# The first token block's 1/rms moved from the input of the first projection to its outputs

## The chip, the cores and the metric

The kernel is one program on one core of a Trainium2 chip. The metric is the device time of one execution in microseconds (us), the median of the runs shown. Engines are named as in the profile: PE (TensorE matmul) and PEld (its weight loads), DVE (VectorE), ACT (ScalarE), POOL (GpSimd), SP (SyncE, which issues most DMAs; SPq is its queue).

## The reference, cut to what matters

One hybrid decoder layer over 2064 tokens (16 meta tokens and 2048 others) of 1024 features, all in fp32:

```python
h = jnp.concatenate([meta, x], axis=1)
hn = rms_norm(h, norm_mix_g[i])              # h * rsqrt(mean(h*h) + eps) * g
proj = hn @ w_in[i]                          # 1024 -> 4 x 512
b_gate, c_gate, v, u = ...                   # the four groups of 512 columns
conv_out = b_gate * causal_dwconv(c_gate * v, conv_w[i])
ssm_out = s5_group_ssm(u, ...)               # diagonal complex state space, GELU, half-GLU
mixed = concat(rms_norm(conv_out, ...), rms_norm(ssm_out, ...))
h = h + mixed @ w_out[i]
hn = rms_norm(h, norm_ffn_g[i])
up = causal_dwconv(hn @ w_up[i], ...);  a, val = up[:D_FF], up[D_FF:]
h = h + (silu(a) * val) @ w_down[i]
y = rms_norm(h, norm_final_g)[:, N_META:]
```

The factor 1/rms of a token is one number for all its features. So it can be multiplied into `h` ahead of `@ w_in`, or into the columns of the product behind it. In `b_gate * dwconv(c_gate * v)` each of the three factors carries it for its own token.

## The kernel before, in words

**Layout.** Features lie on the 128 partitions (8 groups of 128), tokens along the free dimension. The tokens are cut into six quarters q0 to q5 of 344 tokens (`QL`), two to a block; block 0 is q0 and q1. A quarter of x comes as two halves of four feature groups each (tiles `x_c`, 128x1376, 688 KB, from three buffers with the tag `xt`).

**Products.** Each fp32 operand is split into a high part in the format fp32r and a low part that is the rest (`parts`, L245: ACT copies the high part, DVE subtracts for the low part). A product is then three matmuls per feature group: high x high (L138), weight-high x x-low (L139), weight-low x x-high (L142). Weights are loaded in tiles of 128x1024 (`wr_*`, three buffers) and split into `wh_*` and `wl_*` (four buffers each), two tiles ahead of their use (`Stream`).

**Units.** One weight tile times one block is a unit: 48 matmuls of 128x344 into one of three PSUM buffers of two banks (`unit`, L831). The first unit of a block runs its two quarters one after the other (`by_chunk`), so it can begin with q0 alone. `u_block(b)` (L842) has four units, whose outputs (`pu`) go through ACT (L852) in a strided order into `ut`, and from there to DRAM for the state space. `conv_block(b)` (L859) has four groups j of three units: v (`cv`, copied by ACT to `vs`, L865), c (`cc`, multiplied by `vs` into `cvt` on DVE, L870) and b (`cb`, multiplied on DVE into the convolved `tc`, L883). The order is u_block(0), conv_block(0), u_block(2), u_block(1), conv_block(1), conv_block(2), then the output projections, then the gated MLP over three blocks.

**The norm of a quarter.** `prep_x` (L346) loads the two halves; ACT squares them (`sq_c`, L164); DVE adds them up in three steps (L168 to L170); PE sums over partitions (`st_c`, L188); DVE and POOL form (mean + eps) to the power -1/2 (`sv_c`, `sr_c`, L198 and L199); DVE spreads it on a diagonal (`dg_c`, L203); PE broadcasts it (`sb_c`, L206); ACT copies it to `rs_c` (L211). Then DVE forms x times gain times 1/rms in four instructions per half (`t_c`, L240), ACT copies the high part (`h_c`) and DVE subtracts the low part (`l_c`). `t_c` and `sq_c` share two buffers (tag `sq`).

**The coefficients of the state space.** The generator `coefficients` (L375) computes tables from two loads (`sm`, `bc`) on DVE, in some 300 instructions, many of them on 48 columns; its step is taken four times after every unit of block 0 (`after_unit`, L821), in the order of the program, and is finished after the tenth unit. In it are the matmuls `kps` (L576), 16 transposes (`tp`, L590) that ACT copies out (`tq`, L592) and SP stores to `mat_d`, and after them eight copies `tm` (L623) that are stored there too (L624). `tq` and `tm` share two buffers. When the generator is finished its pool `a0` is released. The pool `xf2`, which takes that space from the right end, holds the split tiles of q4: by the program's addresses the first of them, `h_c4_0` (bytes 207,200 to 212,736 of a partition), lies over the second of the two `tq`/`tm` buffers (bytes 207,104 to 209,152).

**Order of work.** The framework that the kernel is written in orders each engine's instructions ahead of time: an engine issues in a fixed order, in which an instruction that is later in the program stands earlier where the engine would otherwise have nothing ready. `prep` and `ssm` are lists of generators from which one or more steps are taken after each unit. q4 and q5, which u_block(2) needs, are prepared one after the other.

```python
    first = [prep_x(q, hc[0]) for q in range(2)]
    next(first[0])
    stream.fill()
    next(first[1])
    ssm.step(1)
    finish_gens(*first)
    u_block(0, hc[0])
```

Of the kernel before, what the change touches and what calls it, by code (L numbers as in the profile page):

```python
# [11 lines left out]
F32 = mybir.dt.float32  # L12
F32R = mybir.dt.float32r
I32 = mybir.dt.int32
AF = mybir.ActivationFunctionType
ALU = mybir.AluOpType

P = 128
# [4 lines left out]
NJ = 8  # L23
# [5 lines left out]
QL = 344  # L29
NQ = L // QL  # L30
QM = 346
# [5 lines left out]
C_MIX = 0  # L37
# [20 lines left out]
def layer_kernel(ctx, tc, xq, pk, w_in, w_glu, w_out, w_up, w_down, ssm_s, ssm_m, y):  # L58
    nc = tc.nc
    V, S, T, G = nc.vector, nc.scalar, nc.tensor, nc.gpsimd  # L60
# [4 lines left out]
    cp = ctx.enter_context(tc.tile_pool(name="cp", bufs=1))  # L65
# [22 lines left out]
    def col(c):  # L88
        return pv[:, c : c + 1]
# [12 lines left out]
    def f32(ap):  # L102
        return ap.bitcast(F32)

    def two(ap):
        return ap.rearrange("p (c t) -> p c t", c=2)

    def tt(out, a, b, op):
        V.tensor_tensor(out, a, b, op=op)  # L109

    def mul(out, a, b):
        tt(out, a, b, ALU.mult)

    def axpy(out, a, s, b):
        V.scalar_tensor_tensor(out=out, in0=a, scalar=s, in1=b, op0=ALU.mult, op1=ALU.add)  # L115

    def load_weights(src, nk, name):
        raw = wp.tile([P, KD, P], F32, tag="wr", bufs=3, name=f"wr_{name}")
        dma(out=raw[:, :nk, :], in_=src)
        return raw, nk, name  # L120
# [23 lines left out]
    def rhs_of(hs):  # L144
        return lambda k, c: (hs[c][k // 4][0][:, k % 4, :], hs[c][k // 4][1][:, k % 4, :])

    def half_tile(n, name, tag="xt", bufs=3):
        return xp_.tile([P, 4, QM], F32, tag=tag, bufs=bufs, name=name)[:, :, :n]

    def hl_tile(n, name, pool=None, tag="xhl", bufs=8):  # L150
        return (pool or xf).tile([P, 4, QM], F32R, tag=tag, bufs=bufs, name=name)[:, :, :n]
# [7 lines left out]
    def sum_squares(groups, n, name):  # L159

        sqs = []
        for i, a in enumerate(groups):
            sq = half_tile(n, f"sq_{name}_{i}", tag="sq", bufs=2)
            S.activation(sq if len(a.shape) == 3 else sq.rearrange("p k (j c) -> p k j c", j=NJ), a, AF.Square)  # L164
            sqs.append(sq)
        sq = sqs[0]
        if len(sqs) == 2:
            tt(sq, sq, sqs[1], ALU.add)  # L168
        tt(sq[:, 0:2, :], sq[:, 0:2, :], sq[:, 2:4, :], ALU.add)
        tt(sq[:, 0, :], sq[:, 0, :], sq[:, 1, :], ALU.add)  # L170
        return sq[:, 0, :]

    def inv_rms(groups, n, name, out=None):


        s = sum_squares(groups, n, name)
        yield
        yield
        return (yield from inv_rms_of(s, 4 * P * len(groups), n, name, out))

    def inv_rms_of(s, nfeat, n, name, out=None, keep=False):
        sl, starts = slices(n)
        nj = len(starts)
        ps = aux_tile(f"st_{name}")
        terms = s if isinstance(s, list) else [s]
        for j, o in enumerate(starts):
            for i, a in enumerate(terms):
                T.matmul(  # L188
                    ps[:sl, j : j + 1], a[:, o : o + sl], ones[:, 0:1], start=i == 0, stop=i == len(terms) - 1
                )  # L190
        return (yield from inv_rms_at(ps[:sl, :nj], starts, nfeat, n, name, out, keep))
# [53 lines left out]
    def parts(t, hi, lo):  # L245

        S.activation(hi, t, AF.Copy)  # L247
        tt(lo, t, f32(hi), ALU.subtract)
# [4 lines left out]
    def load_halves(loads, n, name):  # L253
        xs = []
        for i, src in enumerate(loads):
            t = half_tile(n, f"x_{name}_{i}")
            dma(out=t, in_=src)
            xs.append(t)
        return xs
# [32 lines left out]
    prep, ssm = Side(), Side()  # L292
# [41 lines left out]
    stream = Stream(items)  # L334
# [11 lines left out]
    def prep_x(q, res, other=False, late=None):  # L346


        xs = load_halves((xq[q, :, 0:4, :], xq[q, :, 4:8, :]), QL, f"c{q}")
        yield  # L350
        yield
        rs = yield from inv_rms(xs, QL, f"c{q}")
        kw = dict(pool=xf2, tag="xhl2", bufs=4) if other else {}
        out = []

        def finish_half(t, i):
            hi, lo = hl_tile(QL, f"h_c{q}_{i}", **kw), hl_tile(QL, f"l_c{q}_{i}", **kw)
            parts(t, hi, lo)
            out.append((hi, lo))
            if i == 1:  # L360
                res.append(out)

        for i, t in enumerate(xs):
            yield
            t = scaled(t, C_MIX + 4 * i, rs, QL, f"c{q}_{i}")
            if late is None:
                finish_half(t, i)
            else:
                late.append(lambda t=t, i=i: finish_half(t, i))


    sgn = col(C_SGN)
# [448 lines left out]
    def after_unit(n=1, n_prep=1):  # L821
        if a1 is None:
            ssm.step(4)
            if not ssm.q:
                start_a1()
                prep.add(prep_x(4, hu, other=True), prep_x(5, hu, late=late))
        else:
            ssm.step(n)
            prep.step(n_prep)
# [12 lines left out]
    def u_block(b, hs, last=False):  # L842
        rhs = rhs_of(hs)
        for m in range(4):
            if last and m == 3:
                while len(late) < 2:
                    prep.step()
            ps = unit(rhs, f"pu_{b}_{m}", m == 0 or last and m == 3)
            ut = cvp.tile([P, NJ, 86], F32, tag="ut", bufs=2, name=f"ut_{b}_{m}")
            if last and m == 3:  # L850
                take_late(2)
            S.activation(  # L852
                ut.rearrange("p j (c x) -> p c x j", c=2),
                ps[:, :, :QL].rearrange("p c (x j) -> p c x j", j=NJ), AF.Copy,
            )
            dma(out=u_d[:, m, :, b * 86 : b * 86 + 86].rearrange("j p c -> p j c"), in_=ut)
            after_unit(n_prep=5 if last else 1)

    def conv_block(b, hs, late_after=False, n_prep=1):  # L859
        rhs = rhs_of(hs)  # L860

        for j in range(4):
            pv_ = unit(rhs, f"cv_{b}_{j}", False)
            vs = cvp.tile([P, B2], F32, tag="cs", bufs=3, name=f"vs_{b}_{j}")
            S.activation(two(vs), pv_[:, :, :QL], AF.Copy)  # L865
            after_unit(n_prep=n_prep)
            pc = unit(rhs, f"cc_{b}_{j}", False)
            cv = cvp.tile([P, B2 + 2], F32, tag="cvt", bufs=1, name=f"cvt_{b}_{j}")
            V.tensor_copy(cv[:, 0:2], halo[:, j, :])
            tt(two(cv[:, 2:]), pc[:, :, :QL], two(vs), ALU.mult)  # L870
            V.tensor_copy(halo[:, j, :], cv[:, B2 : B2 + 2])
            tp = cvp.tile([P, B2], F32, tag="cs", bufs=3, name=f"tc_{b}_{j}")
            S.activation(tp, cv[:, 2:], AF.Copy, scale=col(C_CW + 8 + j))
            axpy(tp, cv[:, 1 : B2 + 1], col(C_CW + 4 + j), tp)
            axpy(tp, cv[:, 0:B2], col(C_CW + j), tp)
            after_unit(n_prep=n_prep)
            if late_after and j == 3:
                while len(late) < 2:
                    prep.step()
            pb = unit(rhs, f"cb_{b}_{j}", j == 3)  # L880
            if late_after and j == 3:
                take_late(2)
            tt(two(tp), pb[:, :, :QL], two(tp), ALU.mult)  # L883
            dma(out=mx_d[2 * b : 2 * b + 2, :, j, :].rearrange("q p t -> p q t"), in_=two(tp))
            after_unit(n_prep=n_prep)
# [29 lines left out]
    def finish_gens(*gens):  # L915
        for g in gens:
            for _ in g:
                pass
# [4 lines left out]

    hc = [[] for _ in range(3)]
    hu, late = [], []
    first = [prep_x(q, hc[0]) for q in range(2)]
    next(first[0])
    stream.fill()
    next(first[1])
    ssm.step(1)  # L930
    finish_gens(*first)
    u_block(0, hc[0])
    conv_block(0, hc[0], late_after=True, n_prep=4)

# [122 lines left out]
    def prep_rs(b):  # L1057

        first, ni, _ = BLOCKS[b]
        n = ni // 2  # L1060
        for c in range(2):
            out = cp.tile([P, QM], F32, tag="rsk", bufs=2, name=f"rsk_{b}_{c}")[:, :n]
            s0 = first + c * n
            rs_f[b][c] = yield from inv_rms_from([h_d[:, i * 4 : i * 4 + 4, s0 : s0 + n] for i in range(2)], n, f"f{b}{c}", out)
            yield
# [93 lines left out]
    for i in range(3):  # L1159
        c = C_FW + i * 44 + FT  # L1160
# [175 lines left out]
    for b in range(3):  # L1336
        tb, ni, no = BLOCKS[b]
        n, nn = ni // 2, no // 2
        o = 2 if b else 0
        nz = o + ni  # L1340
        x, act, later = hf[b], {}, deque()
# [138 lines left out]
        else:  # L1480
            s0, _ = y_at(b, 0)
            for i in range(4):
                t = f32(hl_tile(QM, f"acc_{i}", **(xh2 if i < 2 else {})))
                for m in range(2):
                    dma(
                        out=t[:, 2 * m : 2 * m + 2, :nn],
# [7 lines left out]
            for c in range(2):  # L1494
                s = half_tile(nn, f"tail_sum{c}", tag="sq", bufs=4)[:, 0, :]
                for ms in first_pair if c == 0 else [(m,) for m in range(KD)]:
                    down(last, ms, (c,), rows)
                    for m in ms:
                        q = s if m == 0 else z_tile(f"tq_{c}_{m}")[:, :nn]
# [90 lines left out]
```

## Time and profile before

| | |
|---|---|
| median of 3 runs | 2243.06 us (2239.86 to 2243.66) |
| profiled execution | 2245.62 us, of which the span from first to last instruction is 2243.8 us |
| PE busy | 2136.4 us (95%), 13012 matmuls |
| DVE busy | 1678.8 us (75%) |
| ACT busy | 1107.1 us (49%) |
| mean granted TensorE clock | 0.975 |

The rows shown below come from several views. A row of the timeline is start, duration, engine, line, operation, output tile <- input tiles, shape, count, and in brackets the idle time of the engine before it with what ended it. In a table by stretches of time, each stretch has its length, then the busy time and count of PE, PEld, DVE, ACT and POOL, then the granted clock (1.00 is full speed), the DMA share and GB/s. In a row of one tile, three durations in ns are least, median and most, followed by first and last start in us. The ends of matmuls are modelled; the interval between the starts of two matmuls in a row is the better measure of their pace.

### The profile page before, as it was taken

What the parts mean: (1) busy time and instruction counts of PE and PEld (TensorE: products, weight loads), DVE (VectorE), ACT (ScalarE), POOL (GpSimd) and SP (SyncE); (2) the same over time, 40 slices, a digit from 0 to 9 for tenths busy, and PEclk for the clock granted to TensorE, in tenths of its full rate; (3) what the DMA queues carried; (4) which work ended last, traced back from release to release, by engine and by line L of the source; (5) the groups of instructions that cost most, each with busy time, mean ns of one, the idle gap of its engine ahead of it and who ended that gap; (6) DMA issues with size and microseconds to landing.
All of it is one profiled execution on the core that took longest, in us unless ns stands there. A gap on an engine that the chain in (4) does not pass through costs nothing.

```text
span 2243.8 us, 33100 instructions
## 1 busy us (share of the span) xinstructions
PE 2136.4 (95%) x13012; PEld 2072.6 (92%) x13012; DVE 1678.8 (75%) x2495; ACT 1107.1 (49%) x1647; POOL 151.6 (7%) x174
## 2 busy tenths in 40 slices
PE   4999999999899999999999898999999999999997
PEld 3999999989899999999999898999998999999996
DVE  7776498867866797686669686787768779667776
ACT  3234343326523364554556555455555655555554
POOL 0000000000000001101110010100110010110000
PEclk8899999999999999999999999999999999999998
DMA  5475544343376436525554454725554463554463
GB/s 189 119 225 151 144 133 160 129 130 118 107 245 209 139 95 148 122 77 123 131 131 99 135 148 133 202 77 123 129 133 120 126 180 100 131 119 97 101 174 101
DMA packets 174909, 305.85 MB, mean 136 GB/s; under 512 B 32480, under 2 KB 108960, under 8 KB 174624
## 3 DMA queue, kind: packets, MB, share of 16 engines
q1 hardware_dynamic: 154016, 251.98, 36.2%
q0 software_dynamic: 19584, 47.52, 12.6%
q10 hardware_dynamic: 1152, 4.23, 0.5%
q8 instruction: 102, 1.67, 0.3%
q14 instruction: 55, 0.45, 0.1%
HBM read 219.86 MB, written 83.82 MB: 135 GB/s over the span
## 4 chain that ended last, share of the span: by engine, by line
PE 47%; issue 31%; DVE 8%; DMA 7%; POOL 3%; ACT 2%; SPq 0%; POOLq 0%; DVEq 0%; ACTq 0%
PE xy L1349 5%; PE xy L1350 4%; PE xy L1351 4%; PE dn L138 3%; PE dn L139 3%; POOL h_d L1450 3%; PE dn L142 3%; PE pz L1351 2%; PE pz L1350 2%; PE pz L1349 2%; PE po L138 1%; PE po L139 1%; PE po L142 1%; PE pu L139 1%; PE pu L142 1%
## 5 line engine op out<-in xcount | busy, mean ns | idle before, releaser
L109 DVE TENSOR_TENSOR wl_up<-wr_up,wh_up 128x1024 fp32r<-128x1024 f32 x198 | 241.8, 1222 | 155.0 <-ACT wh_up L247 153.1
L138 PE MATMUL dn<-ah,wh_dn 128*128 128x344 f32 (+1 forms) x1024 | 326.9, 323 | 11.7 <-ACT ah L247 8.9
L139 PE MATMUL dn<-al,wh_dn 128*128 128x344 f32 (+1 forms) x1024 | 325.3, 321 | 0.1
L247 ACT ACTIVATE wh_up<-wr_up 128x1024 fp32r<-128x1024 f32 x198 | 209.3, 1058 | 215.1 <-DVE wr_up L109 59.6
L1349 PE MATMUL xy<-h_t,wh_up 128*128 128x344 f32 (+1 forms) x792 | 264.8, 334 | 11.7 <-ACT z L1387 7.3
L1350 PE MATMUL xy<-l_t,wh_up 128*128 128x344 f32 (+1 forms) x792 | 254.9, 322 | 0.0
L1351 PE MATMUL xy<-h_t,wl_up 128*128 128x344 f32 (+1 forms) x792 | 254.6, 321 | 0.0
L142 PE MATMUL dn<-ah,wl_dn 128*128 128x344 f32 (+1 forms) x1024 | 247.1, 320 | 0.0
L138 PEld LDWEIGHTS dn<-ah,wh_dn 128*128 128x128 f32 x1024 | 193.7, 190 | 16.8 <-ACT ah L247 9.7
L1450 POOL DMA_DIRECT2D h_d<-ev x136 | 118.1, 869 | 1271.6 <-ACT ev L1446 1268.3
L139 PEld LDWEIGHTS dn<-al,wh_dn 128*128 128x128 f32 x1024 | 193.9, 189 | 1.3 <-DVE al L109 0.8
L1349 PE MATMUL xy<-h_b,wh_up 128*128 128x344 f32 (+1 forms) x528 | 176.6, 336 | 10.5 <-ACT ev L1446 8.1
L1349 PEld LDWEIGHTS xy<-h_t,wh_up 128*128 128x128 f32 x792 | 150.5, 190 | 30.4 <-ACT z L1394 13.6
L142 PEld LDWEIGHTS dn<-ah,wl_dn 128*128 128x128 f32 x1024 | 177.9, 189 | 0.0
L1350 PE MATMUL xy<-l_b,wh_up 128*128 128x344 f32 (+1 forms) x528 | 169.8, 322 | 0.0
L1351 PE MATMUL xy<-h_b,wl_up 128*128 128x344 f32 (+1 forms) x528 | 168.6, 321 | 0.0
L1350 PEld LDWEIGHTS xy<-l_t,wh_up 128*128 128x128 f32 x792 | 150.9, 191 | 0.0
L1351 PEld LDWEIGHTS xy<-h_t,wl_up 128*128 128x128 f32 x792 | 150.8, 190 | 0.0
L247 ACT ACTIVATE wh_dn<-wr_dn 128x512 fp32r<-128x512 f32 (+1 forms) x144 | 85.5, 594 | 123.5 <-issue 43.5
L115 DVE SCALAR_TENSOR_TENSOR g<-z,pv,g 128x688 f32<-128x688 f32 (+1 forms) x132 | 122.4, 927 | 19.6 <-ACT g L1354 18.9
L109 DVE TENSOR_TENSOR wl_dn<-wr_dn,wh_dn 128x512 fp32r<-128x512 f32 (+1 forms) x144 | 92.5, 645 | 50.8 <-ACT wh_dn L247 49.8
L115 DVE SCALAR_TENSOR_TENSOR v<-z,pneg,v 128x688 f32<-128x688 f32 (+1 forms) x132 | 122.5, 928 | 9.4 <-ACT v L1354 8.2
(394 smaller groups left out, 5377.2 us busy)
## 6 DMA issues: line engine op xcount, KB each, us to landing
wr_up<-in_w_up SPq DMA_DIRECT2D x132, 512.0 KB, 5.2
h_d<-ev POOLq DMA_DIRECT2D x88, 344.0 KB, 7.0
wr_dn<-in_w_down SPq DMA_DIRECT2D x96, 256.0 KB, 2.7
wr_cw<-in_w_in SPq DMA_DIRECT2D x36, 512.0 KB, 4.7
h_d<-ev POOLq DMA_DIRECT2D x48, 336.0 KB, 6.5
x_c<-in_xq SPq DMA_DIRECT2D x16, 688.0 KB, 4.8
wr_dn<-in_w_down SPq DMA_DIRECT2D x48, 192.0 KB, 2.4
xr<-in_xq SPq DMA_DIRECT2D x24, 344.0 KB, 3.9
```

The lines of the kernel that those rows point to most:

```text
L109: V.tensor_tensor(out, a, b, op=op)
L115: V.scalar_tensor_tensor(out=out, in0=a, scalar=s, in1=b, op0=ALU.mult, op1=ALU.add)
L138: T.matmul(ps[c], hi[:, k, :], xh, start=k == 0, stop=False)
L139: T.matmul(ps[c], hi[:, k, :], xl, start=False, stop=False)
L142: T.matmul(ps[c], lo[:, k, :], xh, start=False, stop=k == nk - 1)
L247: S.activation(hi, t, AF.Copy)
L1349: T.matmul(ps, hi[:, j, :], xh[:, j, :], start=start and j == 0, stop=False, **kw)
L1350: T.matmul(ps, hi[:, j, :], xl[:, j, :], start=False, stop=False, **kw)
L1351: T.matmul(ps, lo[:, j, :], xh[:, j, :], start=False, stop=j == 3, **kw)
L1450: G.dma_start(out=h_d[:, m, s0 : s0 + no], in_=ev, accum_op=ALU.add)
```

## The change

For block 0 alone, `raw_x` takes the place of `prep_x`. A half of x is split as soon as it lands: ACT forms the high part as x times gain (four instructions per half, one for each feature group), and DVE forms the low part as x times gain minus the high part in one instruction per group, where there were a product with gain and 1/rms and a subtraction. The norm of the quarter is computed from the same x afterwards, into a kept tile `rs0`. It is multiplied on DVE: into the outputs of the four u units (where ACT copied), into `vs` (where ACT copied), into `vs` once more for c, and into `tp`, the convolved tile, for b. The opening is reordered: the first weight tile is loaded between the two halves of q0, and the steps of q0 and q1 alternate. The tile of `rs0` shares its buffer with the kept 1/rms of the MLP (`rsk`), which becomes one tile for two quarters with one buffer, where it was a tile for each with two.

```diff
+    def rs_tile(name):
+        return cp.tile([P, 2, QM], F32, tag="rsk", bufs=1, name=name)
+
+    rs0 = rs_tile("rs0")[:, :, :QL]
+
+    def raw_x(q, res):
+        xs, out = [], []
+        for i in range(2):
+            xs += load_halves((xq[q, :, 4 * i : 4 * i + 4, :],), QL, f"c{q}{i}")
+            yield
+        for i, x in enumerate(xs):
+            hi, lo = hl_tile(QL, f"h_c{q}_{i}"), hl_tile(QL, f"l_c{q}_{i}")
+            for k in range(4):
+                g = col(C_MIX + 4 * i + k)
+                S.activation(hi[:, k, :], x[:, k, :], AF.Copy, scale=g)
+                V.scalar_tensor_tensor(
+                    out=lo[:, k, :], in0=x[:, k, :], scalar=g, in1=f32(hi[:, k, :]), op0=ALU.mult, op1=ALU.subtract
+                )
+            out.append((hi, lo))
+            yield
+        res.append(out)
+        yield from inv_rms(xs, QL, f"c{q}", rs0[:, q, :])
...
+            by_j = lambda a: a.rearrange("p c (x j) -> p c x j", j=NJ)
+            out = ut.rearrange("p j (c x) -> p c x j", c=2)
+            if b == 0:
+                mul(out, by_j(ps[:, :, :QL]), by_j(rs0))
+            else:
+                S.activation(out, by_j(ps[:, :, :QL]), AF.Copy)
...
-            S.activation(two(vs), pv_[:, :, :QL], AF.Copy)
+            if b == 0:
+                mul(two(vs), pv_[:, :, :QL], rs0)
+            else:
+                S.activation(two(vs), pv_[:, :, :QL], AF.Copy)
...
+            if b == 0:
+                mul(two(vs), two(vs), rs0)
             tt(two(cv[:, 2:]), pc[:, :, :QL], two(vs), ALU.mult)
...
             axpy(tp, cv[:, 0:B2], col(C_CW + j), tp)
+            if b == 0:
+                mul(two(tp), two(tp), rs0)
...
-    first = [prep_x(q, hc[0]) for q in range(2)]
+    first = [raw_x(q, hc[0]) for q in range(2)]
+    next(first[0])
+    stream.raw.append(load_weights(*stream.items.popleft()))
+    next(first[0])
     next(first[0])
     stream.fill()
+    next(first[0])
     next(first[1])
     ssm.step(1)
-    finish_gens(*first)
+    while first:
+        for g in list(first):
+            if next(g, prep) is prep:
+                first.remove(g)
     u_block(0, hc[0])
...
+        rsk = rs_tile(f"rsk_{b}")
         for c in range(2):
-            out = cp.tile([P, QM], F32, tag="rsk", bufs=2, name=f"rsk_{b}_{c}")[:, :n]
+            out = rsk[:, c, :n]
```

More of the change, by code (lines that the diff above doesn't have):

```diff
@@ L851, in u_block @@
                 take_late(2)
[L852 to L855, printed above, removed]
+            by_j = lambda a: a.rearrange("p c (x j) -> p c x j", j=NJ)
[4 more added lines that the diff above has]
+                S.activation(out, by_j(ps[:, :, :QL]), AF.Copy)
             dma(out=u_d[:, m, :, b * 86 : b * 86 + 86].rearrange("j p c -> p j c"), in_=ut)
```

## The prediction, made before the change was run

> **What bounds the kernel now.** I read the table of engines first, then the span cut into stretches, then the timeline of the first 52 us and of 85 to 190 us.
>
> ```profile
> PE 2136.4 (95%) x13012; PEld 2072.6 (92%) x13012; DVE 1678.8 (75%) x2495; ACT 1107.1 (49%) x1647; POOL 151.6 (7%) x174
> ```
>
> ```profile
> 0.00:10.00 10.00, 0.00 (x0) 0.00 (x0) 1.72 (x13) 4.97 (x4) 0.70 (x6) 1.00 0.82 295
> 10.00:20.00 10.00, 2.80 (x8) 1.74 (x8) 7.45 (x13) 3.17 (x3) 0.87 (x1) 1.00 0.94 337
> ...
> 40.00:50.00 10.00, 5.39 (x17) 4.95 (x18) 9.71 (x37) 5.68 (x5) 0.00 (x0) 0.50 0.47 141
> 46.00:86.00 40.00, 40.00 (x243) 39.88 (x243) 38.95 (x146) 14.21 (x12) 0.00 (x0) 0.95 0.47 113
> 86.00:166.00 80.00, 79.66 (x489) 78.43 (x489) 52.34 (x137) 25.44 (x40) 1.83 (x1) 0.91 0.66 192
> 166.00:190.00 24.00, 23.21 (x147) 22.57 (x146) 20.49 (x29) 12.62 (x13) 0.85 (x1) 1.00 0.45 137
> ...
> 206.00:222.00 16.00, 13.28 (x86) 12.69 (x84) 10.68 (x17) 9.11 (x8) 0.85 (x1) 0.97 0.75 186
> ```
>
> PE is busy 95% of the span, and from 46 us it has hardly a gap up to 206 us. So a microsecond that PE starts sooner is a microsecond of the end, unless something PE needs later does not move with it. In the first 46 us PE does little, and two things show there: DMA is nearly full up to 20 us (0.82, 0.94), and DVE is nearly full from 40 to 86 us (38.95 of 40).
>
> ```profile
> 5.59 1.35 ACT L164 ACTIVATE sq_c<-x_c 128x1376 f32<-128x1376 f32 x1 [3.57 <-DMA x_c<-in_xq]
> ...
> 23.15 0.38 SPq L257 DMA_DIRECT2D x_c<-in_xq  x1
> ...
> 24.56 1.23 PE L138 MATMUL pu<-h_c,wh_u 128*128 128x344 f32 x3 [4.53 <-ACT h_c L247]
> ...
> 30.62 1.36 ACT L164 ACTIVATE sq_c<-x_c 128x1376 f32<-128x1376 f32 x1 [1.85 <-DVE l_c L109]
> ...
> 38.25 1.51 PE L206 MATMUL sb_c<-dg_c,ones 115*128 115x344 f32 x2 [2.10 <-DVE dg_c L203]
> 39.80 0.46 ACT L211 ACTIVATE rs_c<-sb_c 128x344 f32<-128x344 f32 x1 [7.83 <-PE sb_c L206]
> 40.30 3.99 DVE L240 SCALAR_TENSOR_TENSOR t_c<-x_c,pv,rs_c 128x344 f32<-128x344 f32 x8 [0.76 <-ACT rs_c L211]
> ...
> 45.84 0.65 PE L139 MATMUL pu<-l_c,wh_u 128*128 128x344 f32 x1 [0.84 <-DVE l_c L109]
> ...
> 49.73 0.49 PE L142 MATMUL pu<-h_c,wl_u 128*128 128x344 f32 x1
> 50.02 0.49 PE L138 MATMUL pu<-h_c,wh_u 128*128 128x344 f32 x1
> ...
> 50.66 0.32 PE L138 MATMUL pu<-h_c,wh_u 128*128 128x344 f32 x1
> 50.82 0.32 PE L139 MATMUL pu<-l_c,wh_u 128*128 128x344 f32 x1
> ...
> 51.66 1.06 ACT L247 ACTIVATE wh_cw<-wr_cw 128x1024 fp32r<-128x1024 f32 x1 [2.97 <-PE pu L139]
> ```
>
> x of q0 is there at 5.6 us, but its products start at 24.56. The second half of q1 is issued only at 23.15, when the first buffer of x has been scaled. Its norm runs from 30.62 to 40.26, its scaling and split to 45.84, and only then does PE run through. The first unit ends at about 51.6, when it frees the weight buffer that ACT waits for.
>
> **The start, part by part.** *Landing of the last half of x.* In the new order its load needs its buffer read by split and Square, about 13 us (Square of 1.35 us, first half at 5.6, and a split of some 2 us each), and stands on SP behind weight tiles. Ahead of it and with it lie at most 0.11 MB of constants, 2.82 of x, 2.62 of five weight tiles and 1.38 for the coefficients: 6.93 MB. By the two rows, 2.95 MB go in the first 10 us and 337 GB/s after that, so it lands at 21.8; without two of the weight tiles and the coefficients (4.5 MB) at 14.6, which the buffer forbids. I take 20.
>
> *Its split.* A high part of 128x344 on ACT is nearest to the `rs_c` row (0.46 us, same shape and function), the low part on DVE to the `t_c` row (8 in 3.99, 0.50 each): the first group is there 1 us after landing, the last after 4 x 0.46 + 0.5 = 2.3 us. The last 12 products of the first unit then run from 21 to about 24 us, at 0.29 (the starts at 49.73 and 50.02, the slow pace) or 0.16 (50.66 and 50.82, the warm one). Before, the unit ended at 51.6. **PE is 27 us ahead** (bounds 24 to 30).
>
> *The norm beside the products.* From Square to 1/rms took 30.62 to 40.26, 9.6 us; from 22.3 that gives 32. The eviction of the first unit waits for it, and PE has three PSUM buffers: two more units of 7.6 us (48 products at 0.16) end at 39. So it costs nothing while 1/rms is ready by about 37; each microsecond later costs one. POOL's power (0.70 and 0.87 us busy in these stretches) and the small matmuls move with it.
>
> *ACT.* Eight copies go, 16 small ones replace four large; ACT is a third busy from 46 to 166, so nothing either way, unless it holds up the first split (under 1 us).
>
> *DVE.* These rows price what is added and removed:
>
> ```profile
> L109 DVE TENSOR_TENSOR gt<-gt,sg 128x688 f32<-128x688 f32 x12 | 18.0, 1498 | 0.3 <-ACT sg L1028 0.3
> ...
> L109 DVE TENSOR_TENSOR xr<-po,xr 128x688 f32<-128x688 f32 x18 | 15.8, 876 | 32.8 <-PE po L142 32.8
> ```
>
> ```profile
> L109 DVE TENSOR_TENSOR wl_up<-wr_up,wh_up 128x1024 fp32r<-128x1024 f32 x198 | 241.8, 1222 | 155.0 <-ACT wh_up L247 153.1
> ```
>
> ```profile
> L109 DVE TENSOR_TENSOR l_c<-t_c,h_c x10: 1584/1592/1595, 44.2 to 229.4; 128x1376 fp32r<-128x1376 f32 x10
> ```
>
> Removed: four subtractions `l_c` of 1.59, 6.4 us. Added: 12 contiguous products of 0.876 (10.5 us), and four into `ut`, whose output order is strided as in `gt` (1.50), so 6.0 (bound below 3.5, at 0.876). Net +10.1 us in the first block. Behind 86 us DVE has 27.7 of 80 us idle, which covers the convolution's share; without cover its 10.5 us would come on PE, which I keep as the far bound.
>
> The Trainium skill, "VectorE: DVE Perf Modes", section "Mode 1× (REGULAR) — the baseline", says that this mode takes fp32 and odd strides alike at one result per cycle; by it the four would cost 3.5 us and the chain below would come 2.5 us sooner. The trace disagrees (1498 against 876 ns for equal counts), and the sum goes by the trace.
>
> *MLP's `rsk`.* One buffer in place of two only matters if a block's norm starts while the last one's is still read; the scaling that reads it is drained first. Zero, bound 10 us (one norm).
>
> **What does not move with PE.** The coefficients run on DVE, and the space of q4's first split tile is free only when the last `tm` is stored.
>
> ```profile
> 0.00:24.00 24.00, 2.83 (x8) 1.74 (x8) 12.61 (x40) 9.44 (x9) 1.57 (x7) 1.00 0.78 282
> 24.00:46.00 22.00, 10.99 (x40) 8.48 (x40) 19.66 (x72) 7.80 (x8) 0.87 (x1) 0.79 0.44 131
> ```
>
> ```profile
> 85.02 11.21 PE L576 MATMUL kps<-w,mats 128*128 128x16 f32 x64
> ```
>
> ```profile
> L624 SPq DMA_DIRECT2D mat_d<-tm x8: 359/360/926, 124.2 to 146.1; - x8
> ...
> DMA to landing us min/median/max: 2.3/3.1/4.9
> ```
>
> ```profile
> 161.79 1.34 ACT L247 ACTIVATE h_c<-t_c 128x1376 fp32r<-128x1376 f32 x1
> ```
>
> ```profile
> 167.43 1.59 DVE L109 TENSOR_TENSOR l_c<-t_c,h_c 128x1376 fp32r<-128x1376 f32 x1
> ...
> 185.17 3.16 DVE L109 TENSOR_TENSOR l_c<-t_c,h_c 128x1376 fp32r<-128x1376 f32 x2
> ...
> 186.09 0.32 PE L138 MATMUL pu<-h_c,wh_u 128*128 128x344 f32 x1
> ```
>
> Up to 86 us DVE was busy 12.6 + 19.7 + 39.0 = 71.2 us, and `kps` started as soon as its inputs were ready. Now that sum is 71.2 - 6.4 + 6.0 + 0.9 (the first `vs`) = 71.7, starting at 6 us with perhaps 4 us of gaps: `kps` at 82. If DVE first takes the work of the three units by which PE is then ahead (three weight splits of 1.22, of the size of the row above, and five products of 0.88: 8 us) it is 90; if it puts off the tables and the sums of q4 that it did early, 76. From `kps` to the last `tm` landed were 146.1 + 3.1 - 85.0 = 64 us, mostly stores of `tq` and `tm` waiting for two buffers, which PE's lead does not shorten. So q4's tile is free at 146 (140 to 154); before it was free at 149 and wanted at 161.8, which hid it. With PE 27 us ahead it is wanted at 135.
>
> From there: q4's split (7.2 us from 161.79 to 169.0; 6 with its input ready), then q5, whose squares need q4's `t_c` buffers: from 169.0 to the low part of its first half (186.8) 17.8 us. q5 is ready at 146 + 6 + 18 = 170. PE wants it 24 products after the start of u_block(2), at 186.1 + 3.8 - 27 = 163. **It waits 7 us** and restarts slowly.
>
> The stretch from 40 to 50 us shows such a restart: clock 0.50, and products at 0.29 us from 45.84 to 50.3 where the warm pace is 0.16, some 15 products at 0.13 lost: 2 us. The Trainium skill, "TensorE: Matmul & The Clock Gate", section "What's actually happening", says that an idle window of about 3.4 us halves the clock and about 3.4 us of work restores it. By that an estimate for each new pause is 1.7 us, and it speaks against starting early with pauses; the trace's 2 us agrees and is what I use.
>
> Sum: 27 - 7 - 2 = 18 us. The profiled execution (2243.8 span, 2245.6 in all) would take 2227.6; it lies 2.6 over the median 2243.06, so I predict **2225 us**. The wait at 206 to 222 us (2.7 us idle) hangs on q3, behind q5 in the same list, and moves along.
>
> **Rivals.**
> *All 27 us stay* (2216): the coefficients come by 76 and the tile by 140, q5 at 164. For it: DVE had 11.4 idle us before 24 us; against: 38.95 of 40 busy behind.
> *The coefficients come still later* (`kps` at 90): q5 is ready at 178, so 15 + 2 of the 27 us are lost and 10 stay; where 7 of the convolution's 10.5 us of products come ahead too, 3 stay. 2236 lies between. For it: DVE full; against: `kps` depends on no product of the later units.
> *The change does not free PE:* the small matmuls of the norm stand ahead of q1's products in PE's fixed order. Then q1's start at 32 and end at 37, 14 us ahead, and q5 is wanted later than it is ready: 2229. Before, `sb_c` did stand there.
> *Slower:* DVE takes the coefficients ahead of q1's sums, so 1/rms comes late and all three PSUM buffers stay full. PE stops at the fourth unit, which began at 66.8 before (51.6 and two units of 7.6). With 1/rms at 65 us and an eviction of 1.5 the lead is gone, and from there it decides; at 71 us the time is 2249. Against: that needs 33 us of coefficients ahead of 3 us of sums.
>
> **How the numbers follow.** Forecast (11 to 24 us gained) 0.47; all stays 0.22; later coefficients 0.17; PE not freed 0.08; slower 0.06. A measurement here tells about 0.2%, 4.5 us. Faster: 0.47 + 0.22 + 0.08 + 0.11 of the third = 0.88; same 0.06; slower 0.06. Range 2213 to 2238: 30 us (upper bound of the lead) to 5 us gained, with the slow case and the end of the third outside. The forecast's own range is 2219 to 2232.
>
> **What would show it.** First unit's last product at about 24 us; `rs0` at about 32; `kps` between 76 and 90; a PE gap of some 7 us at 160 to 170 before q5's products, with a clock near 0.5 after it; a first `h_c` of q4 that starts when the last `tm` has landed. It is wrong if PE has no such gap (2216), or if gaps before 60 us show PSUM full.

## The result: 12 us faster, two thirds of the forecast gain

The changed kernel takes 2231.49 us (median of 5 runs, 2228.09 to 2233.74), the kernel before 2243.66 us beside it (5 runs, 2239.86 to 2247.10). The ratio is 0.9944, 95% interval 0.993 to 0.9957. The forecast was 2225 us with a range of 2213 to 2238: direction and range hold, the time lies at the edge of the forecast's own 2219 to 2232, and of the 18 us some 12 came.

### The profile page after: what moved, and what is told of

It is laid out like the page before. It is cut to its first block, busy times and chain, and to the rows that moved or that the text cites. A ratio compares the mean times of both kernels' runs of the same rounds, so it can differ in the third digit from the quotient of the medians.

```text
span 2232.0 us, 33123 instructions
## 1 busy us (share of the span) xinstructions
PE 2128.2 (95%) x13012; PEld 2065.3 (93%) x13012; DVE 1684.8 (75%) x2507; ACT 1101.2 (49%) x1651; POOL 151.9 (7%) x174
## 4 chain that ended last, share of the span: by engine, by line
PE 44%; issue 32%; DVE 11%; DMA 6%; POOL 3%; ACT 3%; SPq 0%; POOLq 0%; DVEq 0%; ACTq 0%
PE xy L1391 5%; PE xy L1393 4%; PE xy L1392 4%; PE dn L138 3%; PE dn L139 3%; PE dn L142 3%; POOL h_d L1492 3%; PE pz L1391 2%; PE pz L1393 2%; PE pz L1392 2%; PE po L138 1%; PE po L142 1%; PE po L139 1%; DMA wr_up<-in_w_up 1%; PE cc L138 1%
## 5 line engine op out<-in xcount | busy, mean ns | idle before, releaser
L1391 PE MATMUL xy<-h_t,wh_up 128*128 128x344 f32 (+1 forms) x792 | 264.5, 334 | 13.3 <-ACT z L1429 7.5
```

What stands on the lines that cost most here:

```text
L1391: T.matmul(ps, hi[:, j, :], xh[:, j, :], start=start and j == 0, stop=False, **kw)
```

## The profile after

The profiled execution took 2233.74 us with a span of 2232.0, 11.8 less than before. The table of engines and the same stretches as before, of the changed kernel:

```profile
PE 2128.2 (95%) x13012; PEld 2065.3 (93%) x13012; DVE 1684.8 (75%) x2507; ACT 1101.2 (49%) x1651; POOL 151.9 (7%) x174
```

```profile
10.00:20.00 10.00, 9.37 (x48) 8.65 (x49) 8.99 (x16) 10.00 (x14) 0.00 (x0) 1.00 0.91 319
20.00:30.00 10.00, 10.00 (x62) 9.52 (x62) 9.23 (x36) 4.71 (x8) 2.23 (x1) 1.00 0.72 227
...
46.00:86.00 40.00, 39.08 (x254) 38.80 (x252) 39.62 (x92) 6.18 (x6) 0.00 (x0) 1.00 0.35 93
86.00:166.00 80.00, 76.07 (x463) 74.91 (x462) 65.51 (x169) 26.53 (x40) 1.16 (x1) 0.91 0.67 191
166.00:190.00 24.00, 15.55 (x78) 13.84 (x79) 15.39 (x28) 8.36 (x7) 2.05 (x2) 0.72 0.56 154
...
170.00:180.00 10.00, 4.79 (x12) 3.34 (x13) 7.33 (x13) 5.09 (x5) 0.00 (x0) 0.50 0.58 185
```

PE, which was busy 2.80 us between 10 and 20, is busy 9.37 now and without a gap from 20 to 30. What was won there is partly lost later: from 166 to 190 it is busy 15.55 of 24 us at a clock of 0.72, where it had 23.21 before at 1.00. The timeline of the changed kernel shows the opening:

```profile
5.49 1.28 ACT L387 ACT_TABLE_LOAD   x1 [5.49 <-DMA x_c<-in_xq]
...
9.78 0.65 PE L138 MATMUL pu<-h_c,wh_u 128*128 128x344 f32 x1 [9.78 <-ACT wh_u L247]
...
14.99 0.38 SPq L257 DMA_DIRECT2D x_c<-in_xq  x1
...
24.65 0.46 ACT L211 ACTIVATE rs<-sb_c 128x344 f32<-128x344 f32 x1 [4.57 <-PE sb_c L206]
25.01 2.00 ACT L387 ACTIVATE h_c<-x_c,pv 128x344 fp32r<-128x344 f32 x4
...
36.58 0.46 ACT L211 ACTIVATE rs<-sb_c 128x344 f32<-128x344 f32 x1
37.41 1.46 DVE L109 TENSOR_TENSOR ut<-pu,rs 128x688 f32<-128x688 f32 x1
...
39.01 0.39 PE L138 MATMUL pu<-h_c,wh_u 128*128 128x344 f32 x1 [0.41 <-DVE e L411]
...
83.85 11.86 PE L601 MATMUL kps<-w,mats 128*128 128x16 f32 x64 [0.92 <-DVE w L596]
```

x of q0 is there at 5.49, but ACT first loads its table of functions for 1.28 us, which in the kernel before ran at 0.73 while ACT had nothing else to do. The load of x issued at 14.99 is q1's last half. It took 8.4 us to land (the last number of its row among the DMA issues from 14.5 to 15.6 us, below), so it was there at 23.4. Its split started at 25.01, behind the copy of q0's 1/rms (`rs`, 24.65).

```profile
x_c<-in_xq SPq DMA_DIRECT2D x1, 688.0 KB, 8.4
```

The timeline also shows where the lead goes (the row at 158.77 is the first product of u_block(2), which before stood at 186.09):

```profile
141.23 3.98 DVE L240 SCALAR_TENSOR_TENSOR t_c<-x_c,pv,rs_c 128x344 f32<-128x344 f32 x8
...
152.28 0.87 ACT L905 ACTIVATE tc<-cvt,pv 128x688 f32<-128x688 f32 x1 [7.24 <-DVE cvt L109]
153.06 2.58 ACT L247 ACTIVATE h_c<-t_c 128x1376 fp32r<-128x1376 f32 x2
...
156.43 3.09 DVE L109 TENSOR_TENSOR l_c<-t_c,h_c 128x1376 fp32r<-128x1376 f32 x2
158.05 1.36 ACT L164 ACTIVATE sq_c<-x_c 128x1376 f32<-128x1376 f32 x1 [2.41 <-DVE l_c L109]
158.77 0.32 PE L138 MATMUL pu<-h_c,wh_u 128*128 128x344 f32 x1
166.68 0.76 PE L188 MATMUL st_c<-ones,sq_c 128*115 128x1 f32 x6 [3.33 <-DVE sq_c L109]
170.36 1.51 PE L206 MATMUL sb_c<-dg_c,ones 115*128 115x344 f32 x2 [2.92 <-DVE dg_c L203]
175.88 1.23 PE L138 MATMUL pu<-h_c,wh_u 128*128 128x344 f32 x3 [4.01 <-ACT h_c L247]
177.95 0.66 PE L139 MATMUL pu<-l_c,wh_u 128*128 128x344 f32 x1 [0.84 <-DVE l_c L109]
```

PE comes to u_block(2) 186.09 - 158.77 = 27.3 us ahead. Its 24 products of q4 take 3.8 us (186.09 to 189.87 before), so it wants q5 at 162.6, and q5's come at 175.88, with the low part at 177.95. From there to 181.56 products start 0.29 us apart. That q5 was late is seen; why it was 13 us late and not 7, and what would bring the lead back, is what the experiments ask.

## Experiments

Medians below stand beside runs of the kernel before on the same chip. The letters of the theories belong to each group of texts: in the first four A is the storage under q4 and B the load of DVE; in the others A is the chain through q4's and q5's norm.

### The coefficients' long-lived tiles moved away from q4's

```diff
+    al = es_0.enter_context(tc.tile_pool(name="al", bufs=1))
     a0 = es_0.enter_context(tc.tile_pool(name="a0", bufs=1))
...
-            tq = a0.tile([P, 2, P], F32, tag="tq", bufs=2, name=f"tq_{g2}")
+            tq = al.tile([P, 2, P], F32, tag="tq", bufs=2, name=f"tq_{g2}")
...
-                tm = a0.tile([P, 8, 4, H], F32, tag="tq", bufs=2, name=f"tm_{half}_{g4}")
+                tm = al.tile([P, 8, 4, H], F32, tag="tq", bufs=2, name=f"tm_{half}_{g4}")
```

In the same way `mats`, `w1`, `w2`, `av`, `vm`, `mt` and the last three parts of `bc` go to `al`, so that q4's tiles lie over tables that are read for the last time much earlier.

> The changed kernel, with the coefficients' tiles that are in use to the end (the stores' buffers, vm, mt, av and the factors they need) in a pool of their own at the low end of the space, and those that are dead early on top, so that the four split tiles of q4 lie only over dead ones. Theory A (the wait for q5 comes from storage: q4 cannot be split until the last tm is stored): h_c of q4 follows its t_c at 143 instead of 153 us, the low parts are done at about 150 instead of 159.5, and the PE gap from 163 to 178 us shrinks by 9: 2222 us. Theory B (it comes from DVE, which is full from 120 to 150 us and brings q4's t_c late): h_c moves by under 2 us and the time stays at 2230 to 2232.

Measured: 2230.85 us (2224.65 to 2233.18), ratio 0.9944 (0.9929 to 0.9958), the same as without the edit as far as these runs can tell: the interval is 6.5 us wide. Its timeline:

```profile
139.69 3.98 DVE L240 SCALAR_TENSOR_TENSOR t_c<-x_c,pv,rs_c 128x344 f32<-128x344 f32 x8
...
144.73 3.08 DVE L109 TENSOR_TENSOR l_c<-t_c,h_c 128x1376 fp32r<-128x1376 f32 x2
...
148.24 1.23 SPq L257 DMA_DIRECT2D x_c<-in_xq  x1
156.29 1.36 ACT L164 ACTIVATE sq_c<-x_c 128x1376 f32<-128x1376 f32 x1 [2.88 <-DMA x_c<-in_xq]
...
172.07 1.23 PE L138 MATMUL pu<-h_c,wh_u 128*128 128x344 f32 x3 [4.00 <-ACT h_c L247]
```

q4's split ends at 147.8 and not 159.5, so the storage did hold it up, as A says; A's 2222 us did not come. (The split also stands ahead of `tc` on ACT here, 142.91 against 152.54, where in the changed kernel it stands behind it; this run does not tell the two apart.) But q5 comes only 3.8 us sooner, because its second Square waits for x: that half's buffer is free only when q4's half is scaled (within 139.69 to 143.67), its load then stands on SP until 148.24, and it lands 8 us later. One gate was taken away, and the next one, the load of x, held. What q5 won is still there at 290 us, where the first product of the state space, a mark used again below, starts 2.3 us sooner (291.6 against 293.9). The control, the kernel before with this edit alone:

> The kernel before with the same two pools. Theory A: there the storage was free 12 us before q4 wanted it, so nothing changes: 2243, within 3 us. Theory B: the same. A gain here of 5 us or more would say that the layout by itself is worth something and that its effect on the changed kernel is not the storage wait.

2241.80 us (2237.60 to 2246.04), ratio 0.9993 (0.9983 to 1.0003): nothing, as expected, since there PE does not wait for q5.

### The load of DVE: eight products left out, or put on POOL

The first kernel leaves out the products of `vs` and `tp` with 1/rms that read SBUF, so c and b of block 0 lack that factor; the second issues them on POOL.

```diff
-                mul(two(vs), two(vs), rs0)
+                G.tensor_tensor(two(vs), two(vs), rs0, op=ALU.mult)
...
-                mul(two(tp), two(tp), rs0)
+                G.tensor_tensor(two(tp), two(tp), rs0, op=ALU.mult)
```

> The changed kernel without the second product of vs with 1/rms and without the product of tp with it, so without eight DVE instructions of 0.87 us in the first block (7.0 us of DVE); the convolution's output lacks two of its three factors 1/rms. Theory A: the last tm depends on DMA and not on DVE, so the gap stays: 2228 to 2232. Theory B: what DVE is spared reaches q4's and q5's norm: about 2224 to 2226.

> The changed kernel with those eight products on POOL, which is idle 93% of the time; all is computed. Theory A: as skip8, 2228 to 2232, if a product on POOL takes under the 7.6 us of a unit. Theory B: 2224 to 2227. If POOL takes so long that the c and b units wait for it, slower than 2232.

Left out: 2234.85 us (2228.96 to 2237.51), ratio 0.9960 (0.9946 to 0.9975), no faster than the changed kernel. So the 7 us of products on DVE are not what delays q5. In its timeline the split of q4 stands behind the same `tc` and comes later, not sooner:

```profile
154.55 0.87 ACT L903 ACTIVATE tc<-cvt,pv 128x688 f32<-128x688 f32 x1 [7.25 <-DVE cvt L109]
155.33 2.58 ACT L247 ACTIVATE h_c<-t_c 128x1376 fp32r<-128x1376 f32 x2
```

In both kernels this is an order on ACT that was fixed beforehand: `tc` waits for `cvt`, `cvt` for a product of PE, and q4's high parts stand behind it though `t_c` has long been ready (145.2 in the changed kernel, where the storage is free at 149.1, as worked out below).

On POOL: 2247.04 us (2243.35 to 2248.42), ratio 1.0015 (1.0004 to 1.0026), and the gain is gone. The rows of the line that multiplies `tp`, and PE's timeline:

```profile
L909 POOL TENSOR_TENSOR tc<-tc,rs x4: 1592/2172/4262, 70.1 to 166.6; 128x688 f32<-128x688 f32 x4
```

```profile
87.06 13.84 PE L601 MATMUL kps<-w,mats 128*128 128x16 f32 x64 [5.17 <-DVE w L596]
...
188.44 1.23 PE L138 MATMUL pu<-h_c,wh_u 128*128 128x344 f32 x3 [4.01 <-ACT h_c L247]
```

A product takes 1.6 to 4.3 us where DVE takes 0.87. The Trainium skill, "GPSIMD Engine Reference", section "3.1 Elementwise — side-by-side cycle accounting", gives 4497 ns for 2048 fp32 elements against 2293 on DVE; an estimate from it for 688 is 1.5 us, and the trace's fastest, 1592 ns, agrees while its median of 2172 does not; what makes it longer is not shown. `kps` comes 3.2 us later, PE waits 5.17 us there, and q5's products start 12.6 us later than in the changed kernel, close to the 15.6 us by which the median is longer.

### A later start

q1's last half of x is loaded three times over.

```diff
             xs += load_halves((xq[q, :, 4 * i : 4 * i + 4, :],), QL, f"c{q}{i}")
+            if (q, i) == (1, 1):
+                for _ in range(2):
+                    dma(out=xs[1], in_=xq[q, :, 4:8, :])
```

> The changed kernel with the last half of q1's x loaded three times over, so that it lands 4 to 10 us later and PE's first unit ends that much later. Theory A: since q5 is ready at 176 whatever PE does, some 15 us of PE's lead are surplus: the time stays within 3 us of the changed kernel's (2229 to 2234) and the gap at q5 shrinks by as much as the start is late. Rival: PE's start sets the time, each microsecond later costs one: 2236 to 2242.

Measured: 2237.38 us (2230.80 to 2239.99), ratio 0.9968 (0.9956 to 0.9980). Its timeline:

```profile
34.42 2.00 ACT L390 ACTIVATE h_c<-x_c,pv 128x344 fp32r<-128x344 f32 x4 [8.75 <-DMA x_c<-in_xq]
...
176.79 0.32 PE L138 MATMUL pu<-h_c,wh_u 128*128 128x344 f32 x1
...
183.16 0.74 PE L138 MATMUL pu<-h_c,wh_u 128*128 128x344 f32 x3 [0.93 <-ACT h_c L247]
185.23 0.42 PE L139 MATMUL pu<-l_c,wh_u 128*128 128x344 f32 x1 [1.33 <-DVE l_c L109]
```

The time lies in the rival's numbers, outside A's 2229 to 2234, but the edit cost more than I had reckoned: x lands at 34.4 and not 23.4, its split starts 9.4 us later, and by u_block(2) PE is 18.0 us later (176.79 against 158.77). Of these 18.0 us the end loses 5 to 6 (2243.91 x 0.0024 = 5.4). The wait for q5, 13.3 us, has shrunk to 2.6 (183.16 less 176.79 and the 3.8 of q4's products). So about 12 us of PE's lead were surplus, as A says; had each microsecond counted, the time would have been 2249. But A's premise, that q5 is ready at 176 whatever PE does, fails: q5's products come 7.3 us later (183.16 against 175.88). Less the 2 us of slow restart, which this kernel does not have (its clock is 1.00 from 170 to 190), that is what the time loses.

### q4 prepared sooner

q4's norm and scaling may begin before the coefficients are finished; its split waits for the tile. The tiles are moved as above.

```diff
     u_block(0, hc[0])
+    q4 = {}
+    prep.lanes = 2
+    prep.add(prep_x(4, hu, gate=q4), prep_x(5, hu, late=late, after=q4))
     conv_block(0, hc[0], late_after=True, n_prep=4)
```

> q4's norm and scaling are taken into the coefficients' stretch, with the late-live coefficient tiles at the other end; q5 still goes through its norm before its split. Theory A: q4's split ends some 5 us sooner than with the tiles moved alone, but q5's second half of x still stands on SP behind the stores of vm, so q5's products start 0 to 6 us sooner than there (172): 2224 to 2231. If the chain through q4 alone made q5 late, q5 is ready before 163 and the time is 2216 to 2219.

Measured: 2228.48 us (2223.26 to 2238.57), ratio 0.9939 (0.9919 to 0.9959). Its timeline:

```profile
138.27 1.36 ACT L247 ACTIVATE h_c<-t_c 128x1376 fp32r<-128x1376 f32 x1 [0.61 <-DVE t_c L240]
...
145.06 2.83 SPq L257 DMA_DIRECT2D x_c<-in_xq  x1
...
155.60 1.36 ACT L164 ACTIVATE sq_c<-x_c 128x1376 f32<-128x1376 f32 x1 [2.33 <-DMA x_c<-in_xq]
...
171.39 1.23 PE L138 MATMUL pu<-h_c,wh_u 128*128 128x344 f32 x3 [4.01 <-ACT h_c L247]
```

q4's first half is split from 138.27, 15 us sooner than in the changed kernel, and q5's products come 4.5 us sooner, at 171.39. With the tiles moved alone they came at 172.07, so preparing q4 sooner adds 0.7 us; this is A, and q5 was not ready before 163. The second half of q5's x is issued at 145.06 and landed only at 155.6, with DMA full (share 0.96 from 150 to 160), and the norm from Square to split takes the other 16 us.

### q4 and q5 split without their 1/rms as well

The change itself, applied to u_block(2): `raw_more` splits x of q4 and q5 as `raw_x` does, 1/rms goes to a tile that takes the buffer of `rs0` when block 0 is done, and u_block(2)'s outputs are multiplied by it.

```diff
-                prep.add(prep_x(4, hu, other=True), prep_x(5, hu, late=late))
+                prep.add(raw_more(4, hu), raw_more(5, hu, late=late), more_rms(0), more_rms(1))
...
-            if b == 0:
-                mul(out, by_j(ps[:, :, :QL]), by_j(rs0))
+            if b != 1:
+                while b not in rsb:
+                    prep.step()
+                mul(out, by_j(ps[:, :, :QL]), by_j(rsb[b]))
```

> Theory A: the 15 us that PE loses at q5 are the serial chain Square, sum, 1/rms, scaling, split of q4 and then of q5, which began when q4's tile became free; the norm is in it only because x is scaled before it is split. Here q4 and q5 for u_block(2) are also split without 1/rms, and u_block(2)'s four outputs are multiplied by it (4 products of 1.46 us on DVE in place of 4 evictions on ACT). Then q4 is split about 5 us after its tile is free (147 to 153 us), q5 after the last product of the first block (158.6) and its own x. q5's second half of x can be loaded only when q4's first half is split, so it lands at 158 to 163 and its products can follow at 160 to 165, where PE wants them at 162.6. Gap at q5 0 to 4 us in place of 15, lead of PE over the kernel before 23 to 27 us at 180: 2216 to 2222 us. Theory B: the gap is made elsewhere (DVE full from 120 to 150, or the next x halves q2 and q3): the gap at q5 may go, but the time comes back before 220 us, 2228 to 2232.

> Both edits: q4 and q5 split without 1/rms, and the late-live coefficient tiles at the other end of the space so that q4's tile is free some 20 us sooner. Theory A: q4 is split by about 145, q5's x lands by about 155, no gap of PE at q5 (under 2 us): 2213 to 2219 us, and 1 to 4 us under the first edit alone. Theory B: 2228 to 2232.

Alone: 2221.30 us (2218.33 to 2226.14), ratio 0.9906 (0.9890 to 0.9921). With the moved tiles: 2217.74 us (2211.87 to 2218.68), ratio 0.9883 (0.9865 to 0.9900), 14 us under the changed kernel and 26 under the one before. Both are as A expects. The stretches of the second:

```profile
160.00:170.00 10.00, 10.00 (x63) 9.80 (x63) 10.00 (x15) 6.09 (x8) 0.00 (x0) 1.00 0.76 250
170.00:180.00 10.00, 9.99 (x64) 9.50 (x64) 9.04 (x17) 1.41 (x2) 1.20 (x1) 1.00 0.91 226
190.00:206.00 16.00, 12.43 (x75) 11.16 (x74) 12.41 (x19) 5.90 (x6) 0.85 (x1) 1.00 0.61 142
...
260.00:320.00 60.00, 59.23 (x359) 57.53 (x358) 59.43 (x90) 22.73 (x28) 0.00 (x0) 1.00 0.48 158
```

The gap at q5 is gone. How much of the lead reaches the next stage shows in the first product of the state space (`py`), of the kernel before, the changed one and this one:

```profile
L781 PE MATMUL py<-ub,mo x64: 378/381/768, 306.5 to 494.6; 128*128 128x258 f32 x64
```

```profile
L806 PE MATMUL py<-ub,mo x64: 378/381/768, 293.9 to 483.0; 128*128 128x258 f32 x64
```

```profile
L852 PE MATMUL py<-ub,mo x64: 378/381/769, 279.9 to 467.2; 128*128 128x258 f32 x64
```

The leads there are 12.6 and 26.6 us, and the spans are shorter by 11.8 and 28.0. So the opening's 27 us do reach the end when q5 is there.

### q2 and q3 too

The new gap, 3.6 us between 190 and 206 (16 less 12.43; the 7 us in the text below are too many), is q3's norm and split. Here block 1 is treated as block 0 is.

```diff
-    prep.add(prep_x(2, hc[1]), prep_x(3, hc[1], other=True, late=late))
+    prep.add(raw_more(2, hc[1]), raw_more(3, hc[1], late=late, other=True), more_rms(1, 2, 2))
...
-            if b == 0:
-                mul(two(vs), pv_[:, :, :QL], rs0)
+            if b < 2:
+                mul(two(vs), pv_[:, :, :QL], rsb[b])
```

> The version with the moved tiles and raw splits of q4 and q5, and with q2 and q3 of u_block(1) and conv_block(1) split without 1/rms as well (u and convolution outputs of that block multiplied by it, 16 products on DVE more). In the version before, PE waits some 7 us in all between 190 and 206 us for q3's norm, scaling and split. Theory A (the wait is the norm in front of the split): that gap goes and the time is 2209 to 2215 us. Rival: q3's x itself is late (its load waits for a buffer on SP), or DVE, which gets 14 us of products more, holds the outputs: the gap stays or moves on, 2215 to 2222.

Measured: 2217.54 us (2215.55 to 2220.66), ratio 0.9879 (0.9861 to 0.9897), the same as without. Its stretches, its first `py`, and PE's waits in the last stretch:

```profile
190.00:206.00 16.00, 15.52 (x95) 14.87 (x95) 11.95 (x17) 6.14 (x9) 0.00 (x0) 1.00 0.77 186
...
260.00:320.00 60.00, 57.99 (x349) 55.94 (x348) 59.70 (x91) 20.39 (x25) 0.00 (x0) 1.00 0.43 142
```

```profile
L853 PE MATMUL py<-ub,mo x64: 378/381/769, 277.4 to 468.9; 128*128 128x258 f32 x64
```

```profile
269.71 0.42 PE L138 MATMUL cb<-h_c,wh_cw 128*128 128x344 f32 x1 [0.98 <-DVE cvt L109]
...
299.02 0.42 PE L138 MATMUL cb<-h_c,wh_cw 128*128 128x344 f32 x1 [1.02 <-DVE cvt L109]
```

The gap closes (12.43 to 15.52 us busy) and `py` starts 2.5 us sooner, but the last `py` starts 1.7 us later. DVE, full from 260 to 320 already without them (59.43 of 60), has most of the convolution's twelve products of block 1 to do there as well (they start between 233.7 and 331.1); PE is busy 1.2 us less, and waits for `cvt` on DVE, 2.0 us in two waits where it was 0.8 in one. That is the rival: the wait went, and DVE took it back. That the rest up to the last `py` went in the same way is not shown.

## Why the prediction came out as it did

**The lead of 27 us: right.** 27.3 us at u_block(2). But not by the path foretold. The last half of q1's x landed at 23.4 and not 20, and its split waited until 25.01 behind a copy on ACT, so the sign "first unit's last product at 24" did not come. It cost nothing, since PE's fixed order fills with products of the next units that need only what is there (10.00 of 10 us busy from 20 to 30). The forecast had no such filling: that its 27 us held although x came late is luck. 1/rms of q1 came at 36.6 to 37.0, not 32, at the edge of the 37 from which it costs: PE stands still for 0.41 us, until 39.01, which by the times is the wait for the first `ut` (37.41 to 38.87).

**The coefficients: right.** `kps` at 83.85 (forecast 82). The strided product took 1.46 to 1.52 us (forecast 1.50, and not the 0.876 of a contiguous one), and leaving out eight of the others gained nothing.

**When q4 and q5 are ready: the step that failed.** The forecast was q4's tile free at 146, split done at 152, q5 ready at 170, wanted at 163, wait 7 us. The chain of q5 was sized rightly (17.8 us forecast; 159.5 to 177.95 is 18.4), and so was the moment at which PE wants it (162.6). The mis-sized term is q4's split, done at 159.5: 7.5 us later. The row of `tm`'s stores in the changed kernel, and the one issued last among the DMA issues from 144 to 156 us:

```profile
L649 SPq DMA_DIRECT2D mat_d<-tm x8: 359/365/1730, 125.3 to 145.1; - x8
```

```profile
mat_d<-tm SPq DMA_DIRECT2D x1, 256.0 KB, 4.0
```

The last was issued at 145.1 and landed 4.0 us later, at 149.1, where I had taken 146: 3.1 us of the 7.5. Then the split stood on ACT behind `tc`, which waited for `cvt`, and so for a product of PE, until 152.28, and it started at 153.06: 4.0 us more. The rest is the split itself, 6.5 us for 6. So the sign "a first `h_c` of q4 that starts when the last `tm` has landed" did not come. I had worked out when the storage is free, but not what stands ahead on ACT, the engine that writes to it.

**The sum.** 27.3 less 13.3 of wait less about 2 for the low part and the slow pace leaves 12.0, and the span is 11.8 shorter. The wait was 13.3 and not 7; that is the whole difference to 18. The rival "the coefficients come still later" has the nearer time (q5 ready at 178, 15 + 2 of the 27 us lost) but for a cause that did not occur: `kps` was on time. The shared buffer of `rsk` cost nothing that shows, as foretold: the lead is 12.6 us at the first `py` and 11.8 at the end of the span.

**The restart.** 2 us forecast; the products after 177.95 came 0.29 us apart until 181.56, at a clock of 0.50 from 170 to 180. The 3.6 us of that stretch agree with the 3.4 us of work that the Trainium skill, "TensorE: Matmul & The Clock Gate", section "What's actually happening", gives for the way back to full speed.

## What to carry to other kernels

Work moved forward is worth what the next late input leaves of it: find the first place where the sooner engine meets something that does not move with it, and size that by the last gate of the chain, buffers, order on the queue and loads together. Taking away one gate (the storage), or two (q4's late norm as well), brought q5 some 4 us sooner in the trace, which the medians here cannot tell from nothing. What helped was to apply the same change to the input that had become late, since it removes the chain and not one of its waits; it ended where the engine that takes the extra products is full.

## What the runs showed of the hardware

The same product of 128x688 fp32 took 0.87 us on DVE and 1.6 to 4.3 us on POOL beside a busy DVE. From 150 to 160 us DMA stood at a share of 0.96 to 1.05 in several of these kernels (0.82 in the kernel before). A load of 688 KB issued into that took 7.9 us to land in the changed kernel (issued at 149.75), 8.0 with the tiles moved (148.24) and 10.5 with q4 prepared sooner (145.06); in the kernel before, the one issued at 23.15 took 4.3.
